# A DMA-bound average pool: which of two waiting stores goes first

## The chip, the cores and the metric

The kernel runs on one core of one Trainium2 chip. The metric is the device time of one execution in microseconds (us), as a median over runs. The trace covers most of that time: it starts with the first load's issue, and some 1.4 us of it (91.85 us of the profiled run, last landing at 90.46) lie outside.

## The reference

Average pooling over windows of 2 x 2 x 2, cut to what matters:

```python
# x: (8, 32, 32, 32, 32) float32, kernel_size 2
window = x[:, :, 2*i:2*i+2, 2*j:2*j+2, 2*k:2*k+2]
result[:, :, i, j, k] = np.mean(window, axis=(-3, -2, -1))
```

It reads 33.55 MB from HBM, where input and output lie, and writes 4.19 MB to it (the kernel's tiles lie in SBUF); each output is seven additions and a factor.

## The kernel before

The input is 256 rows of 128 KB (batch times channel). The first 128 rows are the first half, one row on each of 128 partitions, loaded in four units of 32 KB a partition. The second half comes in six smaller units: four of 24 KB a partition and two of 16 KB. VectorE (DVE in the traces) sums each unit with three instructions into a result tile, `obuf[0]` or `obuf[1]`.

```python
    for t, k, kb in plan:                 # ten units
        tin = pool_in.tile([P, 32 * KF], F32, tag="tin", name="tin")   # 5 buffers
        ...
        nc.sync.dma_start(out=buf, in_=src)
        pool_unit(buf, t, k, kb)          # VectorE: three sums

    nc.sync.dma_start(out=ov, in_=obuf[0])            # store A: 16 KB a partition

    for queue, k, n, kb in [
        (nc.sync, 0, 4, 3),                           # store B: 12 KB a partition
        (nc.sync, 12, 2, 2),                          # store C: 4 KB a partition
    ]:
        queue.dma_start(out=of[...], in_=obuf[1][...])
```

All transfers are issued by SyncE (SP) into one queue, in program order. A needs units 1 to 4, B units 5 to 8, C units 9 and 10. A loop behind this widens the source patterns of the second half's loads and of B and C to longer contiguous runs, moves the first load ahead of the start barrier, and makes SyncE wait for the stores only at the very end.

Of the kernel before, what the change touches and what calls it, by code (L numbers as in the profile page):

```python
# [12 lines left out]
@with_exitstack  # L13
def pool_rows(
    ctx: ExitStack,
    tc: tile.TileContext,
    x: bass.AP,
    kernel_size: int,
    out: bass.AP,
):  # L20
    nc = tc.nc
    assert kernel_size == 2, "only kernel_size == 2 supported"

    B, C, D, H, W = x.shape
    P = nc.NUM_PARTITIONS
    assert (B * C, D, H, W) == (2 * P, 32, 32, 32)
    add = mybir.AluOpType.add





    xv = x.rearrange("b c d h w -> (b c) (d h w)")[:P]
    ov = out.rearrange("b c d h w -> (b c) (d h w)")[:P]
    xf = x.rearrange("b c d h w -> (b c d h w)")[P * 128 * KF:]
    of = out.rearrange("b c d h w -> (b c d h w)")[P * 16 * KF:]




    pool_in = ctx.enter_context(tc.tile_pool(name="pin", bufs=5))
    pool_out = ctx.enter_context(tc.tile_pool(name="pout", bufs=1))
    obuf = [pool_out.tile([P, 16 * KF], F32, name=f"obuf{t}") for t in range(2)]
    dummy = pool_out.tile([P, 1], F32, name="dummy")


    plan = [
        (0, 0, 32),
        (0, 32, 32),
        (0, 64, 32),  # L50
        (0, 96, 32),
        (1, 0, 24),
        (1, 24, 24),
        (1, 48, 24),
        (1, 72, 24),
        (1, 96, 16),
        (1, 112, 16),
    ]

    def pool_unit(buf, t, k0, kb):  # L60

        od = kb // 8
        a = buf.rearrange("p (o dd e) -> p o dd e", o=od, dd=2)
        b = buf[:, :od * 1024]
        nc.vector.tensor_add(  # L65
            out=b.rearrange("p (o e) -> p o e", o=od), in0=a[:, :, 0], in1=a[:, :, 1])
        bv = b.rearrange("p (e ww) -> p e ww", ww=2)
        c = buf[:, od * 1024:od * 1536]
        nc.vector.tensor_add(out=c, in0=bv[:, :, 0], in1=bv[:, :, 1])  # L69
        cv = c.rearrange("p (j hh k) -> p j hh k", hh=2, k=16)  # L70
        o0 = k0 * KF // 8
        nc.vector.tensor_tensor_reduce(  # L72
            out=obuf[t][:, o0:o0 + od * 256].rearrange("p (j k) -> p j k", k=16),
            in0=cv[:, :, 0], in1=cv[:, :, 1],
            scale=0.125, scalar=0.0, op0=add, op1=add, accum_out=dummy[:, :],
        )

    for t, k, kb in plan:
        tin = pool_in.tile([P, 32 * KF], F32, tag="tin", name="tin")
        buf = tin[:, :kb * KF]  # L80
        if t == 0:
            src = xv[:, k * KF:(k + kb) * KF]
        else:
            src = xf[P * k * KF:P * (k + kb) * KF].rearrange("(p e) -> p e", p=P)
        nc.sync.dma_start(out=buf, in_=src)  # L85
        pool_unit(buf, t, k, kb)


    nc.sync.dma_start(out=ov, in_=obuf[0])


    for queue, k, n, kb in [
        (nc.sync, 0, 4, 3),
        (nc.sync, 12, 2, 2),
    ]:
        queue.dma_start(
            out=of[P * k * KF:P * (k + n * kb) * KF].rearrange("(u p e) -> p u e", u=n, p=P),
            in_=obuf[1][:, k * KF:(k + n * kb) * KF].rearrange("p (u e) -> p u e", u=n),
        )


def kernel(tc: tile.TileContext, x: bass.AP, kernel_size: int, out: bass.AP):
    nc = tc.nc
    pool_rows(tc, x, kernel_size, out)
    tc.close()
    tc.compile()  # L106
# [112 lines left out]
```

## Time and profile before

| | before |
|---|---|
| time, median of 3 runs | 91.96 us (91.9 to 92.06) |
| span of the profile, to the last counted instruction | 86.5 us |
| busy: VectorE | 64.3 us (74%) |
| busy: 16 DMA engines | 99.2% of the span |
| stores land (issue + time to landing) | A 85.5, B 89.2, C 90.5 us |

Issues of DMAs don't count as busy, and the span ends before the stores have landed, so the landings (a transfer has landed when its last completion signal, a semaphore count, is recorded) are worked out from the timeline and the issue list. "DMA share" is the busy share of the 16 engines. The trace also keeps a record of every DMA packet: start, duration, bytes. Where the text says "packet records", the numbers come from there; packets were strung together into engines by matching ends and starts.

### The profile page before, as it was taken

How to read it: one execution, taken by the hardware profiler on the slowest of the kernel's cores; microseconds unless marked ns; L12 is line 12 of the kernel's file. 1: busy time of each engine (PE TensorE's matmuls, PEld its weight loads, DVE VectorE, ACT ScalarE, POOL GpSimd, SP SyncE). 2: the span in 40 equal slices, each digit the busy share in tenths (PEclk: the TensorE clock that was granted, in tenths of full speed). 3: DMA queues.
4: the chain of work that ended last, by engine and by line, in shares of the span. 5: the costliest groups of instructions: out<-in, count | busy, mean ns of one | idle time of the engine just before them, and what ended most of it. 6: DMA issues, size and time to landing. Idle time of an engine off the chain costs nothing.

```text
span 86.5 us, 90 instructions
## 1 busy us (share of the span) xinstructions
DVE 64.3 (74%) x40; POOL 0.2 (0%) x4
## 2 busy tenths in 40 slices
DVE  0000049992999749992999999799689949999992
POOL 0000000000000000000000000000000000000000
DMA  8979998899979999899889998889988899899999
GB/s 242 424 333 455 485 485 379 379 455 485 485 318 424 470 485 424 364 424 606 364 364 409 591 455 364 364 364 523 568 364 364 364 485 424 349 439 303 432 439 402
DMA packets 1264, 36.44 MB, mean 421 GB/s; under 512 B 176, under 2 KB 176, under 8 KB 176
## 3 DMA queue, kind: packets, MB, share of 16 engines
q1 hardware_dynamic: 1264, 36.44, 99.2%
HBM read 33.55 MB, written 4.19 MB: 436 GB/s over the span
## 4 chain that ended last, share of the span: by engine, by line
DMA 71%; DVE 26%; issue 0%; SPq 0%; DVEq 0%
DMA tin<-in_x_dram 71%; DVE tin L65 14%; DVE tin L69 8%; DVE obuf L72 4%; SPq L85 0%; DVE dummy L72 0%; DVEq L106 0%
## 5 line engine op out<-in xcount | busy, mean ns | idle before, releaser
L65 DVE TENSOR_TENSOR tin<-tin 128x4096 f32<-128x4096 f32 (+2 forms) x10 | 35.7, 3570 | 19.9 <-DMA tin<-in_x_dram 19.9
L69 DVE TENSOR_TENSOR tin<-tin 128x2048 f32<-128x2048 f32 (+2 forms) x10 | 18.6, 1865 | 0.3
L72 DVE CUSTOM_DVE_ANT_1 obuf<-tin 128x1024 f32<-128x1024 f32 (+2 forms) x10 | 10.1, 1011 | 0.3
L72 DVE DVE_READ_ACCUMULATOR2_ANT dummy<- 128x1 f32 x10 | 0.8, 82 | 0.0
L200 POOL MEMSET const-bfloat16-1.0<- 128x1 bf16 x1 | 0.1, 101 | 0.0
L200 POOL MEMSET const-uint8-127<- 128x1 uint8 x1 | 0.1, 101 | 0.0
L200 POOL MEMSET const-float32-0.0<- 128x1 f32 x1 | 0.1, 99 | 0.2 <-issue 0.2
L200 POOL MEMSET const-float32-1.0<- 128x1 f32 x1 | 0.1, 99 | 0.0
## 6 DMA issues: line engine op xcount, KB each, us to landing
tin<-in_x_dram SPq DMA_DIRECT2D x4, 4096.0 KB, 25.6
tin<-in_x_dram SPq DMA_DIRECT2D x4, 3072.0 KB, 34.5
tin<-in_x_dram SPq DMA_DIRECT2D x2, 2048.0 KB, 25.7
out_dram<-obuf SPq DMA_DIRECT2D x1, 2048.0 KB, 29.7
out_dram<-obuf SPq DMA_DIRECT2D x1, 1536.0 KB, 12.6
out_dram<-obuf SPq DMA_DIRECT2D x1, 512.0 KB, 5.5
```

Of the source, the lines that this page charges most:

```text
L65: nc.vector.tensor_add(out=b.rearrange("p (o e) -> p o e", o=od), in0=a[:, :, 0], in1=a[:, :, 1])
L69: nc.vector.tensor_add(out=c, in0=bv[:, :, 0], in1=bv[:, :, 1])
L72: nc.vector.tensor_tensor_reduce(out=obuf[t][:, o0:o0 + od * 256].rearrange("p (j k) -> p j k", k=16), in0=cv[:, :, 0], in1=cv[:, :, 1], s ...
L200: nc = _bacc.Bacc("TRN2", target_bir_lowering=False, num_devices=1)
```

## The change

The 12 KB store of the second half (B) is issued first, the 16 KB store of the first half (A) behind it, then C.

```diff
-    nc.sync.dma_start(out=ov, in_=obuf[0])
-    for queue, k, n, kb in [
-        (nc.sync, 0, 4, 3),
-        (nc.sync, 12, 2, 2),
-    ]:
-        queue.dma_start(
+    for k, n, kb in [(0, 4, 3), (12, 2, 2)]:
+        nc.sync.dma_start(
             out=of[P * k * KF:P * (k + n * kb) * KF].rearrange("(u p e) -> p u e", u=n, p=P),
             in_=obuf[1][:, k * KF:(k + n * kb) * KF].rearrange("p (u e) -> p u e", u=n),
         )
+        if k == 0:
+            nc.sync.dma_start(out=ov, in_=obuf[0])
```

As B must wait for the eighth unit and SyncE issues in order, A is now also issued after that.

## The prediction

> **What bounds the kernel now.** I read the page first: which engine is busy, then the DMA part, then the issues with their times to landing.
>
> ```profile
> span 86.5 us, 90 instructions
> DVE 64.3 (74%) x40; POOL 0.2 (0%) x4
> ...
> q1 hardware_dynamic: 1264, 36.44, 99.2%
> ...
> DMA tin<-in_x_dram 71%; DVE tin L65 14%; DVE tin L69 8%; DVE obuf L72 4%; SPq L85 0%; DVE dummy L72 0%; DVEq L106 0%
> ...
> out_dram<-obuf SPq DMA_DIRECT2D x1, 2048.0 KB, 29.7
> out_dram<-obuf SPq DMA_DIRECT2D x1, 1536.0 KB, 12.6
> out_dram<-obuf SPq DMA_DIRECT2D x1, 512.0 KB, 5.5
> ```
>
> VectorE is idle for a quarter of the span, and the 16 DMA engines are busy for 99.2% of it: this is a kernel of transfers. All of them go through one queue, issued by SyncE. Note that the span of 86.5 us ends with the instructions that the profile counts, shortly after VectorE's last one; the stores are still running then, so the span is not the kernel's end. For that I need the issue of each store plus its time to landing. The issues stand in the timeline:
>
> ```profile
> 49.10 0.08 DVE L72 DVE_READ_ACCUMULATOR2_ANT dummy<- 128x1 f32 x1
> ...
> 55.80 0.58 SPq L89 DMA_DIRECT2D out_dram<-obuf  x1
> ...
> 76.46 0.08 DVE L72 DVE_READ_ACCUMULATOR2_ANT dummy<- 128x1 f32 x1
> ...
> 76.57 8.96 SPq L96 DMA_DIRECT2D out_dram<-obuf  x2
> ...
> 84.85 0.08 DVE L72 DVE_READ_ACCUMULATOR2_ANT dummy<- 128x1 f32 x1
> ```
>
> The store of the first half (call it A, 2048 KB) is issued at 55.80, directly behind the last load, though its data was ready at 49.2. The 12-KB-a-partition store of the second half (B, 1536 KB) is issued at 76.57, when the eighth of the ten units is summed; the last store (C, 512 KB) at 85.0, when the tenth is (the line with x2 merges B and C; the view of that line gives 85.0 as C's start). Adding the times to landing: A lands at 55.80 + 29.7 = 85.5, B at 76.57 + 12.6 = 89.2, C at 85.0 + 5.5 = 90.5. B and C land 3.7 and 1.3 us after the transfer ahead of them, although they were issued 12.6 and 5.5 us before: they stand in a line. Is there a hole anywhere in that line? The view by windows, whose last two columns are the DMA engines' busy share and GB/s, goes past the end of the span:
>
> ```profile
> 1.00:12.00 11.00, 0.00 (x0) 0.00 (x0) 1.00 1.05 429
> 12.00:30.00 18.00, 15.90 (x8) 0.00 (x0) 1.00 1.01 437
> 30.00:55.80 25.80, 21.92 (x13) 0.00 (x0) 1.00 1.01 437
> ...
> 80.00:85.00 5.00, 4.83 (x6) 0.00 (x0) 1.00 1.00 426
> 85.00:86.50 1.50, 0.00 (x0) 0.00 (x0) 1.00 0.98 418
> ```
>
> No. The narrow windows wobble, because a packet's bytes are booked at one moment, so I went to the trace's single packet records and strung them together engine by engine. From the first packet (1.02 us) to the last (90.05 us) no engine has a gap over 0.06 us between two packets. The durations are nearly constants: a 32 KB load packet takes 1.213 us (median), a 48 KB one 1.83, a 16 KB packet of A 0.611, a 12 KB packet of B 0.460, a 4 KB packet of C 0.159. The switches also show there: A's packets begin at 79.73 on the first engine done with loads, B's at 84.59, C's at 88.24.
>
> So the end is a sum: first packet at 1.0, then about 89.0 us of packets back to back on each engine, 0.4 us from the last packet to the last landing (90.05 to 90.46), and 1.5 us from there to the measured 91.96, outside the trace.
>
> **What the Trainium skill says.** "DMA: Bandwidth & Descriptors", Queues, rings and completion order: a DMA copy is split over its queue's rings, one on each engine, and each engine consumes its descriptors in ring order. The trace agrees: A, issued at 55.8, moves nothing before 79.7, when the loads ahead are through. That makes the order of issue the order of transfer, which is all that the change touches. The same page, Specifications, gives 435 GB/s as the fabric's ceiling and about 0.6 us as first-byte latency for this kind of queue. The windows show 426 to 437 GB/s, so the ceiling is reached. For the latency the trace has its own number: the first load's issue starts at 0.00 and its first packet at 1.02 us, of which 0.39 is the issue. "Perfetto Trace Analysis", DMA Instruction — HWDGE, says that the profiled window of a DMA instruction leaves out the data movement; here A's window is 0.58 us and its landing comes 29.7 us after.
>
> **The change part by part.**
>
> Nothing is removed or added: the same ten loads and three stores, the same shapes and bytes, the same VectorE program. The comparison of the two instruction orders shows one swap on SyncE, A and B, and no other difference on any engine except line numbers. Three things move.
>
> 1. A's issue moves from 55.8 to behind B's. SyncE now meets B's wait first (for the eighth unit), so A is issued when B's issue is done: 76.57 + 0.6 = about 77.2. The issues of stores take 0.562 to 0.623 us. Nothing else waits for A, and the loads had all been issued by 55.75, so no load moves.
>
> 2. The line behind the loads changes from A, B, C to B, A, C. Eight packets each per engine: A is 8 x 0.611 = 4.9 us, B 8 x 0.460 = 3.7, C 8 x 0.159 = 1.3. The sum is 9.9 in either order. B should then land at 85.5 - 4.9 + 3.7 = 84.3, A at 89.2, C at 90.5 as before.
>
> 3. The slack changes. This is the only part that can cost anything, since a sum with no hole stays the same as long as none is opened. Before, A lay ready for 24 us and B arrived 84.59 - 76.57 = 8.0 us before its first packet was due. Now B must be there at 79.73, 3.2 us after its issue starts. With the 1.0 us that the first load needed from issue to packet, it is there at 77.6: 2.1 us to spare (an estimate; B's destination has four runs of 3 KB in a partition, yet its issue takes no longer than A's). A, there by 78.2, is due at 79.73 + 3.7 = 83.4: 5 us to spare. C, issued at 85.0 and there at 86.0, is due at 88.24, as before: 2.2 us to spare.
>
> Sum: 0 us on the path. VectorE's last unit needs load 10, which is ahead of all stores in both orders, so C's issue stays at 85.0.
>
> **The rivals.**
>
> *A hole before B.* If B needs over 3.2 us from issue to first packet, the engines run dry between the loads and the stores, and each further microsecond is one more at the end; at 4.2 us the kernel would be at about 93.0. For it: B is now issued into a nearly empty line, and its 512 short runs may take longer to be turned into descriptors than a load's few rows. Against it: 0.562 to 0.623 us per store issue, and 1.0 us measured for the first load. I give a visible hole 5%, and one above 1.8 us 1%.
>
> *A gain from the small store going first.* B lands 4.9 us earlier, and one might hope that the tail shrinks. But the end is C's landing, C waits for VectorE's tenth unit and for both other stores, and their sum is unchanged. It could only gain if the packets got faster. They are constants to the nanosecond for the stores in this trace, at 427 to 429 GB/s for A and B over 16 engines; I see nothing for it. The gain would be 0.1 to 0.2 us, 91.8.
>
> *VectorE becomes the bound.* C's issue hangs on VectorE's last reduction at 84.9. If VectorE came later by more than the 2.2 us that C has to spare, C would arrive late. Against it: its last four units run without a wait from 70.39 to 84.9, and nothing in the change touches their loads. No effect.
>
> *Another pattern of reads beside writes.* The engines drift apart by some 0.5 us, so at the switch from loads to stores some read while others write. The switch is there in both orders, A's or B's packets after the loads. No effect above 0.1 us.
>
> **Range and chances.** Predicted is the old median less nothing: 91.96, rounded to 91.95. The three runs before span 0.16 us. A range of 91.75 to 92.25 covers that spread, a rival of 0.2 us to the fast side and a small hole on the slow side. A change of 2% is 1.84 us; to the fast side the packets' sum forbids it, to the slow side it needs a hole of that size. Hence 0.01 faster, 0.98 within 2%, 0.01 slower.
>
> **What would show it right or wrong.** Step 1: A's issue stands at about 77.2. Step 2: time to landing is about 7.7 us for B (84.3), 12.0 for A (89.2) and 5.5 for C (90.5); packet durations unchanged. Step 3: no gap in the packet records at 79.7. Wrong would be: a DMA share that falls between 78 and 81 us, a C that lands after 90.8, or A's packets longer than 0.611 us when they run between B and C.

## The result, and the profile after

The changed kernel takes 91.34 us (6 runs, 91.31 to 91.44) beside 91.93 us for the kernel before (6 runs, 91.74 to 92.09). The ratio is 0.9937, 95% interval 0.9924 to 0.9951: within 2%, but clear of noise, and outside the predicted range. Ratios are the mean time of one kernel's fast runs over that of the other's of the same rounds, so not quite the ratio of the medians quoted.

The issues in the changed kernel's timeline (start, duration):

```profile
76.58 0.62 SPq L91 DMA_DIRECT2D out_dram<-obuf  x1
77.26 0.58 SPq L96 DMA_DIRECT2D out_dram<-obuf  x1
...
84.98 0.57 SPq L91 DMA_DIRECT2D out_dram<-obuf  x1
```

B at 76.58, A at 77.26, C at 84.98, as predicted. Next the last part of the changed kernel's page, KB and time from issue to landing:

```profile
tin<-in_x_dram SPq DMA_DIRECT2D x2, 2048.0 KB, 25.5
out_dram<-obuf SPq DMA_DIRECT2D x1, 2048.0 KB, 11.4
out_dram<-obuf SPq DMA_DIRECT2D x1, 1536.0 KB, 7.3
out_dram<-obuf SPq DMA_DIRECT2D x1, 512.0 KB, 5.0
```

The page of the kernel before had this for the two last loads:

```profile
tin<-in_x_dram SPq DMA_DIRECT2D x2, 2048.0 KB, 25.7
```

B lands at 83.8, A at 88.7, C at 89.9: each about half a microsecond ahead of the prediction, so the gain was made before the first store. And the two last loads, which the change does not touch, landed 0.2 us sooner; the median of two is their mean, so if one of them is unchanged, the other came 0.4 us sooner. The semaphore records say which: the tenth load landed 5.33 us after the ninth in the kernel before (75.26 to 80.59) and 4.90 us after it in the changed one (75.27 to 80.17).

The view by windows shows the same where the tenth load runs. The last two columns are DMA share and GB/s; first the kernel before:

```profile
76.60:80.00 3.40, 3.37 (x2) 0.00 (x0) 1.00 0.95 342
78.00:80.00 2.00, 1.97 (x2) 0.00 (x0) 1.00 0.99 320
...
80.00:84.00 4.00, 3.93 (x4) 0.00 (x0) 1.00 1.01 434
```

and the changed kernel:

```profile
76.60:80.00 3.40, 3.37 (x2) 0.00 (x0) 1.00 0.95 402
78.00:80.00 2.00, 1.97 (x2) 0.00 (x0) 1.00 1.00 422
...
80.00:84.00 4.00, 3.93 (x5) 0.00 (x0) 1.00 1.04 440
```

Between 78 and 80 us the engines are busy for 0.99 of the time before the change and for all of it after, but before it they move 320 GB/s, after it 422. Busy, and slow: there is no gap to find, the packets themselves are longer. The packet records of these two microseconds, one line for each of three engines (start, end, ns, bytes):

```
before   78.069-80.018  1949  32768        changed  78.004-79.231  1227  32768
before   78.367-79.827  1460  32768        changed  78.260-79.487  1227  32768
before   78.475-80.100  1625  32768        changed  78.490-79.717  1227  32768
```

In the kernel before, the last load packet of every one of the 16 engines took 1.43 to 1.95 us, some of the ones just before it up to 1.53; in the changed one all of both took 1.227. I call the excess over 1.227 us, summed over the load packets that start after 74.9 us and divided by 16, the **stretch**: 0.515 us per engine before, 0.00 after. The last packet of all ended at 90.05 before and at 89.54 after. So the half microsecond is the stretch; the rest of the 0.59 us between the medians is not resolved in one trace of each.

### The profile page after: what moved, and what is told of

The parts are those of the page before. It is cut to its first block, busy times and chain, and to the rows that moved or that the text cites. A ratio compares the mean times of both kernels' runs of the same rounds, so it can differ in the third digit from the quotient of the medians.

```text
span 86.5 us, 90 instructions
## 1 busy us (share of the span) xinstructions
DVE 64.3 (74%) x40; POOL 0.2 (0%) x4
## 4 chain that ended last, share of the span: by engine, by line
DMA 71%; DVE 26%; issue 0%; SPq 0%; DVEq 0%
DMA tin<-in_x_dram 71%; DVE tin L65 14%; DVE tin L69 8%; DVE obuf L72 4%; SPq L85 0%; DVE dummy L72 0%; DVEq L103 0%
```

## The experiments

The first question was what in the old order stretches the last load's packets. **Theory 1**: A, issued at 55.8, lies ready in the line while the loads run. **Theory 2**: it is the neighbourhood, 16 KB packets of A right behind loads. **Theory 3**: issuing B while A is already in the line disturbs the loads. The waits on VectorE's count that the edits add are on constants (each of the ten units adds three); their diffs below are a summary of what the edit does to the wait list, not its code. Each group of runs had a chip of its own, and the kernel before ran beside it: 91.96 us beside the first three runs and 92.16, 91.89 and 91.91 beside the later groups. So compare the ratios across groups, not the times.

**Order A, B, C, with A issued late.** The kernel before, with one line's effect added: A's issue waits for the eighth unit.

```diff
 (store A)  on_wait=[]
+(store A)  on_wait=[DVE >= 24]
```

> The order A, B, C of the kernel before, with one thing changed: A (the 16 KB store of the first half) waits for the eighth unit and is issued at about 76.6 us instead of 55.8, with B right behind at 77.2. In the kernel before, the last one or two load packets of every engine (of the last load, 77 to 80.3 us) took 1.43 to 1.95 us instead of 1.23, and the last load landed at 80.59; with B first they took 1.227 and it landed at 80.17. Theory 1 (A lying ready in the line behind the loads stretches the last loads): no stretch here, last load lands at about 80.2, time about 91.4. Theory 2 (16 KB packets of A right behind the loads stretch them, B's 12 KB packets do not): stretch as before, 80.6, time about 91.95. Theory 3 (issuing B while A is already in the line stretches them): A is in the line from about 77.6 on, B's issue ends at 77.8, so stretch as before or part of it, 91.7 to 91.95.

91.47 us beside 91.96, ratio 0.9943 (0.9919 to 0.9967); stretch 0.000. Its issues, and its windows:

```profile
76.62 0.35 SPq L89 DMA_DIRECT2D out_dram<-obuf  x1
77.02 8.56 SPq L96 DMA_DIRECT2D out_dram<-obuf  x2
```

```profile
78.00:80.00 2.00, 1.97 (x2) 0.00 (x0) 1.00 0.93 393
...
80.00:84.00 4.00, 3.93 (x5) 0.00 (x0) 1.00 1.04 446
```

(Bytes and busy time of a packet are booked together, so a narrow window can be short of both, as here: 393 at a share of 0.93 is full speed.) A goes first again, and the gain is there in full. So the order of the stores doesn't matter within the noise: what counts in the change is that it delayed A's issue by 21 us. Theories 2 and 3 fall.

**A early, B issued late.** The kernel before, B waits for the ninth unit.

```diff
-(store B)  on_wait=[DVE >= 24]
+(store B)  on_wait=[DVE >= 27]
```

> The kernel before with one thing changed: B waits for the ninth unit, so it is issued at about 80.7 us instead of 76.6, when the loads are over; A is issued at 55.8 as before. Theory 1 (A lying ready): stretch of the last load packets as before, last load lands at 80.6, time about 91.95. Theory 2 (16 KB packets right behind the loads): the same, 91.95. Theory 3 (B's issue while A is in the line): no stretch, lands at 80.2, time about 91.4; the stretch could also move to whatever runs at 81 us.

92.0 us, ratio 0.9999; stretch 0.489. Its issues and its window:

```profile
55.94 0.58 SPq L89 DMA_DIRECT2D out_dram<-obuf  x1
80.91 4.76 SPq L96 DMA_DIRECT2D out_dram<-obuf  x2
```

```profile
78.00:80.00 2.00, 1.97 (x2) 0.00 (x0) 1.00 0.83 303
```

B is issued when the loads are over, and they were stretched all the same. Theory 3 falls a second time.

**An eighth of A early.**

```diff
-    nc.sync.dma_start(out=ov, in_=obuf[0])
+    nc.sync.dma_start(out=ov[:, :512], in_=obuf[0][:, :512])
     ... store B ...
+    nc.sync.dma_start(out=ov[:, 512:], in_=obuf[0][:, 512:])
```

> A split in two: its first 2 KB of each partition (256 KB in all) are issued at 55.8 behind the last load, the other 14 KB behind B at about 77.2; order A's eighth, B, rest of A, C. Theory 1 (something lying ready behind the loads): the last load's packets are stretched, by the full 0.4 us if any store lying there does it, by much less if it goes with its bytes; time 91.9 or 91.5. Theory 2 (16 KB packets next to loads): little or no stretch, about 91.4 plus what the 2 KB packets cost. Theory 3 (B's issue while a store lies in the line): full stretch, about 91.9.

91.94 us, ratio 0.9988 (0.9958 to 1.0018); stretch 0.279. Nearly all of the gain is lost with an eighth of the bytes lying there. Part of the loss is something else: eight 2 KB packets (0.084 us each) and eight of 14 KB (0.535) take 0.06 us more than eight of 16 KB. Stretch and small packets make 0.34 us; the last packet ended some 0.6 us later than in the changed kernel, and the rest is not resolved in one trace. (Some expectations below give this run's stretch as about 0.35; the packet records give 0.279.)

**How late is late enough?** Two issue times between 55.8 and 76.6, by waiting for the first or the second of the eighth unit's sums:

```diff
+(store A)  on_wait=[DVE >= 22]      # in the second kernel: 23
```

> Order A, B, C with A issued at about 73.8 us (A waits for the first of the eighth unit's three sums), B at 76.6. The first runs left theory 1: a store that lies in the line behind the loads stretches the last load's packets. What is open is when it has to be there. If the engines look ahead of the packet that they move by about one packet or two (theory 1a), A in the line from about 74.8 is early enough: full stretch, some 0.5 us per engine in packets of the last load, last load lands 5.3 us after the ninth, time about 91.95. If it has to lie there longer, over some packets of loads (theory 1b): no stretch or part of it, lands 4.9 us after the ninth, time about 91.4.

> As the run before, with A issued at about 75.6 us (it waits for the second of the eighth unit's sums), so in the line from about 76.6, when the last but one packet of the last load starts on every engine (76.7 to 77.3). Theory 1a: stretched in part or in full, 91.6 to 91.95; theory 1b: no stretch, 91.4. At 76.6 it was not stretched at all, so somewhere between the two the edge must be.

92.0 us (ratio 0.9991, stretch 0.513) and 91.89 us (ratio 0.9984, stretch 0.457). The issues and the window of the second:

```profile
75.58 0.35 SPq L89 DMA_DIRECT2D out_dram<-obuf  x1
76.58 8.98 SPq L96 DMA_DIRECT2D out_dram<-obuf  x2
```

```profile
78.00:80.00 2.00, 1.97 (x2) 0.00 (x0) 1.00 0.99 336
```

One microsecond decides. Counted back from the first packet of A, the store issued 4.1 us ahead (75.58, first packet 79.70) stretches the loads almost in full, the one issued 2.6 us ahead (76.62, first packet 79.20) not at all. (Half a microsecond of the 4.1 is the stretch itself, which put the first packet off; the issues lie 1.04 us apart.) It does not have to lie there long, as theory 1a of these runs has it. That the engines look ahead is the reading behind that theory; the runs show the times only.

**Fewer bytes.** The eighth became a 32nd, 512 B a partition (the edit above with 128 in place of 512).

> A split: its first 512 B of each partition (64 KB in all, 4 KB per engine) are issued behind the last load, the rest behind B. With 2 KB of each partition (16 KB per engine) the stretch was about 0.35 us per engine beside 0.5 with all of A. Theory 1c (the loads give way to the bytes that lie ready, up to some limit): at 27 GB/s per engine 4 KB is 0.15 us, so the stretch is 0.1 to 0.2 us, time about 91.55 to 91.75 with the cost of the small packets. Theory 1d (the turn from loads to a waiting store costs a fixed time): stretch 0.35 or more, time about 91.9.

91.54 us, ratio 0.9943; stretch 0.037, less than either theory said. With 4, 16 and 128 KB (all) of A per engine lying there it was 0.04, 0.28 and 0.5 us: it grows with the bytes, but not in proportion.

**What kind of transfer?** Three runs took the changed kernel and put a superfluous 2 KB a partition behind the last load: a load, a copy from SBUF to SBUF, a copy from HBM to HBM. (The first of them ran in the group with 92.16 us for the kernel before, the other two in that with 91.89.)

```diff
+    spare = pool_out.tile([P, 512], F32, name="spare")       # HBM copy: a DRAM tensor
+    nc.sync.dma_start(out=spare, in_=xv[:, :512])            # SBUF copy: in_=obuf[0][:, :512]
```

> The changed kernel (B, A, C, all issued from 76.6 on) with a superfluous load of 2 KB per partition (256 KB of the input to a spare tile) issued behind the last load, where the store of 2 KB lay in the earlier run. It costs its own 8 packets per engine, about 0.67 us, whatever happens. Theory 1 for anything that lies there: the last load's packets are stretched by 0.35 us too, time about 92.35. Theory 1s (it must be a store, which reads SBUF and writes to HBM): packets of the last load keep their 1.227 us, time about 92.0.

> The changed kernel with a superfluous copy of 2 KB per partition from SBUF to SBUF lying behind the last load. So far, for 2 KB per partition lying there: a store (SBUF to HBM) stretched the last load's packets by 0.28 us per engine, a load (HBM to SBUF) by 0.04. Theory R (it is the reading of SBUF that the engines begin early, ahead of loads whose data are still on the way): stretch about 0.28 here. Theory W (it is the coming write to HBM): about 0.04. Time in either case longer than the changed kernel's by the copy's own packets, some 0.7 us, so about 92.0 (W) or 92.3 (R).

> The same with a superfluous copy of 2 KB rows from HBM to HBM lying behind the last load, the fourth of the four kinds. Theory R (early reading of SBUF): no SBUF is read, stretch about 0.04 us. Theory W (the coming write to HBM): about 0.28.

Times 92.19, 92.34 and 92.18 us (ratios 1.0018, 1.0055, 1.0030); stretches 0.043, 0.224 and 0.172, beside 0.279 for the store. These were inconclusive: the HBM copy, stretching six engines of 16, lies between what the two theories expected. So they were run again with 12 KB a partition (3072 for 512 above), and with a store of 12 KB of A early to compare.

> The changed kernel with a superfluous load of 12 KB per partition (instead of 2 KB) behind the last load. With 2 KB lying there the stretch of the last load's packets per engine was 0.28 us for a store, 0.22 for an SBUF copy, 0.17 for an HBM copy (in 6 engines of 16 only), 0.04 for a load: too near to each other to tell a cause, in one look each. With 12 KB, if only the store's own reading or writing matters: about 0.0 here, time about 95.1. If anything lying there does it in proportion to its bytes: 0.3 or more, 95.4.

> The same with an SBUF to SBUF copy of 12 KB per partition. Theory R (early reading of SBUF while the last loads are under way): the full 0.45 to 0.5 us. Theory W (the coming write to HBM): 0.2 or less, as no HBM is written.

> The same with an HBM to HBM copy of 12 KB rows. Theory R: 0.2 or less, as no SBUF is read. Theory W: 0.45 to 0.5 us. If both of them stretch fully, and the load does not, neither theory alone is right.

> The store to compare these with: 12 KB per partition of A early, behind the last load, then B and the last 4 KB of A from 76.6 on. Both theories: 0.45 to 0.5 us per engine, time about 91.95.

Times 95.61, 95.65, 95.58 and 91.92 us. From the packet records, the stretch of the last load's packets, and the excess of the 12 KB packets over 0.460 us, also per engine:

| 12 KB a partition behind the last load | reads | writes | stretch of the last load | excess of 12 KB packets |
|---|---|---|---|---|
| load | HBM | SBUF | 0.00 | 0.55 |
| HBM copy | HBM | HBM | 0.00 | 0.42 |
| SBUF copy | SBUF | SBUF | 0.51 | 0.00 |
| store (part of A) | SBUF | HBM | 0.35 | 0.00 |

With 12 KB the kinds separate, in one trace of each: what reads SBUF stretched the load ahead of it, wherever it wrote; what reads HBM didn't. (The store's 0.35 is below the 0.45 to 0.5 expected of it and below the SBUF copy's 0.51; why is not shown.) And the two that read HBM suffer themselves: their own last packets, between 81 and 83.6 us, just ahead of B, which has been in the line since about 77. Windows of the load, of the SBUF copy and of the HBM copy, in this order:

```profile
78.00:80.00 2.00, 1.93 (x3) 0.00 (x0) 1.00 1.02 434
81.00:83.60 2.60, 2.57 (x2) 0.00 (x0) 1.00 0.96 321
```

```profile
78.00:80.00 2.00, 1.97 (x2) 0.00 (x0) 1.00 0.82 311
81.00:83.60 2.60, 2.57 (x2) 0.00 (x0) 1.00 1.00 425
```

```profile
78.00:80.00 2.00, 1.97 (x2) 0.00 (x0) 1.00 0.91 387
81.00:83.60 2.60, 2.56 (x2) 0.00 (x0) 1.00 0.99 354
```

And of the store, 12 KB a partition of A early:

```profile
78.00:80.00 2.00, 1.97 (x2) 0.00 (x0) 1.00 0.84 330
80.00:84.00 4.00, 3.93 (x5) 0.00 (x0) 1.00 1.00 427
```

Divided by the share, as above, these are 425 and 334 GB/s for the load, 379 and 425 for the SBUF copy, 425 and 358 for the HBM copy, 393 and 427 for the store. The slow place moves with the turn from reading HBM to reading SBUF. That is also why the three superfluous transfers cost about the same, although the superfluous load was expected at 95.1 us: it was spared at 79 us and paid between 81 and 83.6. It also fits the 2 KB load and HBM copy, though no run tests that: they put B off, so that it was issued 3.4 and 3.6 us ahead of its first packet, between the 2.6 us that did no harm and the 4.1 us that did.

**A store between two loads.** The changed kernel with A's eighth issued between the ninth and the tenth load.

```diff
+        if (t, k) == (1, 112):
+            nc.sync.dma_start(out=ov[:, :512], in_=obuf[0][:, :512])
         nc.sync.dma_start(out=buf, in_=src)
...
-            nc.sync.dma_start(out=ov, in_=obuf[0])
+            nc.sync.dma_start(out=ov[:, 512:], in_=obuf[0][:, 512:])
```

> The changed kernel with the first 2 KB per partition of A taken out and issued between the ninth and the tenth load (the rest of A behind B); it is the run with 2 KB early, moved one load forward. The rest lies behind B, so nothing lies behind the last load until 76.6. Theory 2a (a store is read early and the loads before it pay, wherever it lies, and nothing is given back): packets of the ninth load are stretched by 0.28 us per engine, the last packet ends at about 89.9, time about 91.75. Theory 2b (the loads behind the store take the lost time back, because the engines look ahead past the store to them): stretch too or none, but the sum is that of the changed kernel plus 0.07 for small packets, last packet 89.65, time 91.4 to 91.5.

91.55 us, ratio 0.9967 (0.9947 to 0.9986); packets of the ninth load were stretched by 0.016 us, those of the tenth by 0.05, and the last packet ended at 89.65, where theory 2b put it. So the same 2 KB a partition that stretched the load ahead of it by 0.28 us when it stood behind the last one hardly stretched a load when another stood behind it. In time it is 0.19 us above the changed kernel on the same chip (next run); 0.06 of that are the small packets, and the two ratios' intervals overlap. Why the ninth load was not stretched is not shown.

**The changed kernel once more**, on the chip of the run above.

> The changed kernel itself once more, beside these on one chip: about 91.35, ratio 0.993 to 0.995, last load's packets at 1.227 us, last packet ends at about 89.55.

91.36 us beside 91.89, ratio 0.9952 (0.9929 to 0.9975); stretch 0.00, last packet at 89.57. Holding A back in the old order (ratio 0.9943) is the same within noise. No version here beats the changed kernel.

## Why the prediction was wrong

*The bound, and "the end is a sum".* Right. The engines have no gap of note in either kernel, and the end moved by what the sum of packet times lost.

*The packet times as constants.* **This is the step that failed.** The prediction gave the load packets by their median, 1.213 us, called the durations "nearly constants" and took "about 89.0 us of packets back to back" to hold in any order. The last load's packets were no constants: in the kernel before they held 0.515 us per engine of stretch, which the median of 640 packets hides (their mean is 1.243 us, and 1.231 in the changed kernel; the difference, 0.012 us times 40 packets an engine, is the half microsecond). The view by windows had shown it as well, in a line that the prediction cut: 342 GB/s from 76.6 to 80 us ("426 to 437" leaves it out). The prediction put such dips down to how bytes are booked; the changed kernel's 402 in the same window shows that most of it was real.

*Part 1, A's issue moves to 77.2 "and nothing else waits for A".* The time was right (77.26). That nothing waits for A is true and beside the point: something was held up by A lying there.

*Part 2, the sum of the stores.* Nearly right: 9.9 us in either order. B's packets took 0.466 us in place of 0.460, 0.05 us in all. The landings of all three stores are 0.5 us ahead of those predicted, the stretch again. The sign "packet durations unchanged" of step 2 is the one that caught the error; none of the three signs named under "wrong would be" came (C landed at 89.94, and A's packets kept a median of 0.611).

*Part 3, slack as "the only part that can cost anything".* B was there in time: no gap at its first packet, 2.65 us after its issue. But the part looked for the harm in a late issue and never asked what an early one costs. Short slack was the gain.

*The rival of reads beside writes.* It named the right place, the turn from loads to stores, and dismissed it because "the switch is there in both orders". The switch is; what differs is how long before it the store was issued.

*The other rivals.* That of a gain named the right condition, "if the packets got faster", but looked for it among the stores' packets and gave it 0.1 to 0.2 us; it was the last load's packets, by 0.5. "A hole before B" and "VectorE becomes the bound" were rightly dismissed (it is VectorE's last three units, not four, that run without a wait after 70.39).

*What the runs showed in place of the failed step.* The last load's packets took up to 0.5 us more per engine where a transfer that reads SBUF stood right behind it and had been issued some 4 us or more ahead of its first packet: 0.46 to 0.52 us for all of A, 0.35 and 0.51 for 12 KB a partition, 0.28 and 0.22 for 2 KB, 0.04 for 512 B. The time wasn't regained. With all of A issued 2.6 us ahead, or with a load behind the 2 KB, they didn't. A reading of this, argued and not shown: the reading side of an engine runs ahead of its writing side, comes to the store while load data are still on their way from HBM, and fetches SBUF data that no one needs yet. The Trainium skill, "DMA: Bandwidth & Descriptors", Two DMAs through the same engine are not ordered, says that the read and write sides are separate queues and pipelined, which fits. Why the loads pay for it, and why they don't with another load behind the store, stays open; the second of these is also a case that the reading alone does not explain.

## What to carry to other kernels

A store that lies ready behind loads is not always free while it waits: in a DMA-bound kernel, try issuing the first store behind the last loads just in time (here some 2.6 us ahead), for example behind an issue that has to wait anyway. Don't take "no gaps" and a busy share near 1 for full speed; compare GB/s by windows, and the mean and the longest packets with the median. And before calling a sum independent of order, check that its terms are the same wherever they stand.

## What the Trainium skill lacked or had wrong

- "DMA: Bandwidth & Descriptors", Queues, rings and completion order, tells that each engine consumes its descriptors in ring order, but not that a descriptor further back already acts on those ahead: a store in the line stretched the last load by 0.515 us per engine, most of the 0.59 us between 91.93 and 91.34.
- The same page, Rules for kernel authors, advises to issue a DMA early to overlap it with compute. It lacks an exception for a store behind loads: 91.47 us with A issued at 76.6, 91.96 with A at 55.8.
- The same page, Specifications, gives about 27 GiB/s per engine. The packets show 32768 B in 1.213 us, 27.0 GB/s, which is 25.2 GiB/s; it fits the page's own ceiling of 435 GB/s over 16 engines.
- "Perfetto Trace Analysis", DMA Engine Tracks, says that slices show actual busy time. It doesn't say that a stretched packet counts as busy: share 0.99 at 320 GB/s. The page's advice under Identifying the Most-Contended Engine, to use HBM utilization instead of occupancy for DMA, would have found it if taken by windows (over the whole span the page of each kernel gives 421 and 424 GB/s).
